# FFN up projection from seven block products instead of eight, with h split at the down projection

## The chip, the cores and the metric

The kernel runs on one core of one Trainium2 chip, in one launch. The metric is the device time of the launch in microseconds (us). A core has a matrix engine (TensorE, PE in the rows), a vector engine (VectorE, DVE), an activation engine (ScalarE, ACT), a general engine (GpSimd, POOL) and a queue that issues loads (SyncE, SP). Each runs its own instructions in the order in which they were put down; semaphores order them against each other. SBUF is the memory that all engines read and write, PSUM the one that matrix products land in.

## The reference, cut to what matters

The reference is one layer of a hybrid decoder for 512 prompt tokens and 64 sample tokens (8 sequences of 8), 576 tokens in all. The change touches only the gated feed-forward network (FFN) at its end:

```python
def conv_ffn(xn, conv_prev, w_up, conv_w, conv_b, w_down):
    t_len = xn.shape[1]
    a, b = jnp.split(xn @ w_up, 2, axis=-1)
    ext = jnp.concatenate([conv_prev.astype(a.dtype), a], axis=1)
    y = conv_b + conv_w[0] * ext[:, 0:t_len] + conv_w[1] * ext[:, 1:t_len + 1] + conv_w[2] * ext[:, 2:t_len + 2]
    h = jax.nn.silu(y) * b
    return h @ w_down, ext[:, -(CONV_WIDTH - 1):]
```

`xn` is the normalized [576, 1024] activation, `w_up` is [1024, 5632], `w_down` [2816, 1024], all FP32. The second result, the last two columns of `a` of each sequence, is an output too. A final norm follows.

## The kernel before

**Products.** FP32 precision comes from splitting each operand into a high part (`hi`, rounded to the matrix format fp32r) and the rest (`lo`), and adding three products: hi by hi, hi by lo, lo by hi. So each block of 128 rows by 128 columns of a weight costs three matmuls per token range, with the weight block as stationary operand and the tokens as moving operand. ScalarE makes the high part (L161), VectorE subtracts it from the raw weight for the rest (L164). A chunk of weights is one load by SyncE into `wr` (three buffers), usually 1024 by 128: eight blocks, one tile of 128 partitions by 1024. Its parts `wh` and `wl` have two buffers each. `fetch(i)`, called as chunk i begins, cuts chunks i and i+1 and loads i+2 and i+3.

**The stage before.** After the merge of the three mixers and the output projection, `x1` holds the residual; `xh2`, `xl2` its split, times the norm's gain but without the norm's factor for each token, `rst`. That factor is known only some 10 us after the first FFN matmul; so it is applied to the products.

**FFN up.** 2816 columns are 22 pairs: 128 gate columns `a`, 128 value columns `b`. For each f of the 22, `gemm` runs `a` over two token ranges (SPLIT, 256 and 320 tokens) and `b` over two of 288 (EVEN): 8 blocks, 3 products and 2 ranges each, 96 matmuls for a pair. VectorE takes `a` out of PSUM times `rst` into `ae` (L1159, L1161); the width-3 convolution is three VectorE instructions over 592 columns (L1184 to L1186), ScalarE applies SiLU (L1187), GpSimd multiplies by `rst` into `yr` (L1189, L1190), VectorE multiplies by `b` from PSUM (L226), and the result is split at once: `hh` on ScalarE (L1194), `hl` on VectorE (L1195). GpSimd also keeps the last columns of `a` (L1170, L1171) and issues behind them one copy of a cache within DRAM (L183), the side copies.

**FFN down.** For each of 8 blocks of 128 output columns, `down` (L1249) runs over the 22 blocks of h in three chunks (8, 7, 7 blocks), two token ranges side by side; the last block runs its ranges one after the other, so that the end can begin early. Transposes, the final norm and the output follow.

The order on each engine is the order of the code; a few instructions are put elsewhere by hand with `issue_after`. In the up loop the cut of the next chunk, called by `fetch`, stands in VectorE's order between the instructions that take results out.

## Time and profile before

| | us |
|---|---|
| median of 3 runs | 1325.38 (1325.1 to 1326.37) |
| span of the profiled execution | 1324.9 |
| the profiled execution outside its span | about 0.5 |
| PE busy | 1305.0 (99%) |
| DVE, ACT, POOL busy | 601.6, 464.3, 242.4 |
| first FFN up matmul starts | 886.99 |
| first FFN down matmul starts | 1171.16 |

The span is what the profiler saw from the first to the last instruction. The time of a run is taken around the program, and the median stands about 0.5 us above the span. A group row ("L164 DVE ... x43 | 52.6, 1222") gives line, engine, operation, output and inputs with their shapes, count, then busy time in us and mean duration of one in ns, and after a second bar the idle time of the engine just before these instructions and what ended it. A timeline row gives start, duration, engine, line and operation. PE instructions overlap: a matmul's own duration (297 ns) is longer than the distance from one to the next, and it is that distance which counts for time.

### The profile page before, as it was taken

The numbers are of one execution on the slowest core, as the hardware profiler recorded it, in microseconds if no ns is written. First come the engines' busy times: TensorE is split into PE (matmuls) and PEld (weight loads), VectorE is DVE, ScalarE is ACT, GpSimd is POOL, SyncE is SP. The second block draws the span as 40 slices with busy tenths as digits, with TensorE's granted clock in tenths as the row PEclk, the third lists the DMA queues.
The fourth block names the chain that finished last, engine by engine and source line by source line (L and its number), as shares of the span: only waits on it lengthen the run. The fifth ranks groups of instructions, "written<-read, shape, count | busy, mean of one in ns | idle before, by whom it ended". The sixth has DMA issues, their size and how long they took to land.

```text
span 1324.9 us, 23686 instructions
## 1 busy us (share of the span) xinstructions
PE 1305.0 (99%) x9903; PEld 1257.5 (95%) x9903; DVE 601.6 (45%) x1004; ACT 464.3 (35%) x899; POOL 242.4 (18%) x398
## 2 busy tenths in 40 slices
PE   8899999999999999999999999999999999999997
PEld 6899999999999999998988889999999999999997
DVE  5754564433453333162633366435555555532223
ACT  6554553534321222242433343433222222222223
POOL 4320211022410112041311110122121212200000
PEclk9999999999999999999999999999999999999999
DMA  7232432355443557266676415363455555444333
GB/s 218 65 116 68 144 115 69 96 178 158 131 141 95 163 159 220 73 184 190 182 217 204 154 31 167 100 225 118 145 164 162 162 167 157 148 129 149 91 88 116
DMA packets 220582, 187.44 MB, mean 141 GB/s; under 512 B 7900, under 2 KB 216393, under 8 KB 219700
## 3 DMA queue, kind: packets, MB, share of 16 engines
...
q8 instruction: 78, 1.28, 0.4%
...
q10 hardware_dynamic: 2, 0.00, 0.0%
...
## 4 chain that ended last, share of the span: by engine, by line
PE 94%; DVE 2%; ACT 2%; issue 1%; DMA 1%; POOL 0%; SPq 0%; POOLq 0%; DVEq 0%; ACTq 0%
PE g L207 63%; PE g L1249 8%; PE g L395 8%; PE h L1249 2%; PE h L936 1%; PE s L805 1%; PE s L207 1%; PE s L864 1%; PE s L828 1%; PE s L820 1%; PE s L881 1%; PE h L869 1%; PE s L611 0%; DVE bb L475 0%; PE s L591 0%
## 5 line engine op out<-in xcount | busy, mean ns | idle before, releaser
L207 PE MATMUL g<-xl,wh 128*128 128x288 f32 (+2 forms) x1664 | 494.1, 297 | 0.0
L207 PE MATMUL g<-xh,wh 128*128 128x288 f32 (+2 forms) x1664 | 494.1, 297 | 0.0
L207 PE MATMUL g<-xh,wl 128*128 128x288 f32 (+2 forms) x1664 | 492.8, 297 | 1.1 <-DVE wl L164 1.1
L161 ACT CAST wh<-wr 128x1024 fp32r<-128x1024 f32 (+3 forms) x181 | 184.4, 1019 | 485.8 <-PE g L207 287.8
L164 DVE TENSOR_TENSOR wl<-wr,wh 128x1024 fp32r<-128x1024 f32 (+3 forms) x179 | 227.1, 1268 | 252.9 <-ACT wh L161 252.2
L207 PEld LDWEIGHTS g<-xh,wl 128*128 128x128 f32 x1664 | 313.7, 189 | 3.3 <-issue 1.4
L207 PEld LDWEIGHTS g<-xl,wh 128*128 128x128 f32 x1664 | 314.1, 189 | 2.3 <-issue 2.0
L207 PEld LDWEIGHTS g<-xh,wh 128*128 128x128 f32 x1664 | 314.2, 189 | 1.1 <-issue 0.7
L395 PE MATMUL g<-wh,xh 128*128 128x256 f32 x224 | 72.1, 323 | 2.5 <-DVE vs L400 2.5
L1249 PE MATMUL g<-hh,wl 128*128 128x288 f32 (+2 forms) x286 | 72.2, 297 | 0.0
L1249 PE MATMUL g<-hh,wh 128*128 128x288 f32 (+2 forms) x286 | 72.0, 297 | 0.0
L395 PE MATMUL g<-wl,xh 128*128 128x256 f32 x224 | 71.5, 319 | 0.0
L1249 PE MATMUL g<-hl,wh 128*128 128x288 f32 (+2 forms) x286 | 71.5, 295 | 0.0
L395 PE MATMUL g<-wh,xl 128*128 128x256 f32 x224 | 71.4, 320 | 0.0
L395 PEld LDWEIGHTS g<-wh,xh 128*128 128x128 f32 x224 | 52.3, 233 | 5.7 <-DVE vs L400 2.7
L395 PEld LDWEIGHTS g<-wl,xh 128*128 128x128 f32 x224 | 52.3, 234 | 0.7 <-issue 0.7
L395 PEld LDWEIGHTS g<-wh,xl 128*128 128x128 f32 x224 | 52.4, 234 | 0.0
L1249 PEld LDWEIGHTS g<-hh,wl 128*128 128x128 f32 x286 | 49.8, 189 | 0.0
L1249 PEld LDWEIGHTS g<-hh,wh 128*128 128x128 f32 x286 | 49.6, 189 | 0.0
L1249 PEld LDWEIGHTS g<-hl,wh 128*128 128x128 f32 x286 | 49.6, 189 | 0.0
L1159 DVE TENSOR_TENSOR ae<-g,rst 128x256 f32<-128x256 f32 x44 | 18.6, 425 | 64.0 <-PE g L207 64.0
L226 DVE TENSOR_TENSOR yr<-yr,g 128x288 f32<-128x288 f32 x44 | 18.1, 451 | 49.8 <-POOL yr L1189 49.8
...
## 6 DMA issues: line engine op xcount, KB each, us to landing
...
```

Source lines behind the costliest of these rows:

```text
L161: S.copy(hi[:, :n], self.raw[:, :n])
L164: self.cut_at = E.tensor_tensor(lo[:, :n], self.raw[:, :n], hi[:, :n].bitcast(F32), op=OP.subtract)
L207: T.matmul(ps[:, :t1 - t0], a[:, k, c:c + 128], b(n)[:, t0:t1], start=(n == 0 and j == 0), stop=(n == len(ks) - 1 and j == 2))
L226: return lambda ps, t0, t1: V.tensor_tensor(t[:, t0:t1], t[:, t0:t1], ps, op=OP.mult)
L395: mm = T.matmul(dst, a, b[:, n % 4, :], start=(n == 0 and j == 0), stop=(n == 7 and j == len(seq) - 1))
L805: T.matmul(sp[:, nk * n:nk * n + nk], qT[r, p, 128 * t:128 * t + 128], kT[r, p, k0:k0 + nk], start=True, stop=True)
L820: T.transpose(pt[:, 128 * n:128 * n + 128], s4[:, h, 128 * kb:128 * kb + 128], ident)
L828: T.matmul(po[64 * hh:64 * hh + 64, 128 * x:128 * x + 128], vt[:, blocks[kb], 64 * (2 * p + hh):64 * (2 * p + hh) + 64], pts[:, (2 * x + h ...
L864: T.transpose(pk[:, 128 * n:128 * n + 128], kt[:, 2 * half + n // 2, 128 * (n % 2):128 * (n % 2) + 128], ident)
L869: T.matmul(sp[32 * b:32 * b + 32, 0:128], qz[:, p, 32 * b:32 * b + 32], kT[:, n, p, :], start=(r == 0 and p == 0), stop=(r == NR[g] - 1 an ...
L1159: V.tensor_tensor(ae[:, 2 + t0:258 + t0], ps[:, :256], rst[:, t0:t0 + 256], op=OP.mult)
L1249: T.matmul(q[:, :t1 - t0], a[:, k, :], b[n][:, t0:t1], start=(n == 0 and j == 0), stop=(n == NF - 1 and j == 2))
```

## The change

The gate and value columns of one pair form a 2 by 2 block matrix: the rows of the weight are split into blocks 0 to 3 and 4 to 7, the columns into `a` and `b`. The tokens are split into two halves of 288. The [tokens] by [rows] times [rows] by [columns] product then has eight block products, and in Winograd's form of Strassen's method it needs seven, with sums before and after:

- **Two plain pairs.** The first two pairs (NF0 = 2) stay as they were, but for the convolution's first step, which moves to ScalarE. Beside them `sums_x`, called four times for two block rows each, forms the seven combinations of x. They hold the norm's factor `rst` already (`scalar_tensor_tensor` with gain and `rst`, 2 instructions of 576 columns a call); two sums each on GpSimd and VectorE, seven high parts on ScalarE, seven rests on VectorE, all 288 wide.
- **20 pairs as units.** For each unit GpSimd forms the weight sums t1 to t4 (128 by 512 each). `part` cuts seven weight operands of 512 columns: high part on ScalarE (L147), rest on VectorE (L149), each into one of four buffers, three products ahead. A product is 4 blocks by 3 matmuls of 288 tokens: 12; seven are 84 for a pair, against 96. The seven products stay in PSUM and are combined: copies s1, s5 on ScalarE, five sums on VectorE with one operand from PSUM (L1334 to L1341, L1344, L1345), one of 288 from SBUF on GpSimd (L1339).
- **h.** GpSimd multiplies SiLU by `hb` into an FP32 h (L1349, L1350); the split into `hh` and `hl` moves behind the last up product: 22 high parts on ScalarE (L1359), 22 rests, 17 on VectorE and 5 on GpSimd (L1360).
- **Everywhere** weights are cut in tiles of 512 columns with four buffers each instead of 1024 with two. Raw weight chunks of the units alternate between `wr` and a second pool. The down projection (L1415) runs its first two output blocks third by third, side by side.

VectorE's order for one pair. Before (`wr`, `wh`, `wl` are raw weight, high part and rest; `ae` the extended gate column, `yr`, `hh`, `hl` the result and its split):

```order
L164 TENSOR_TENSOR wl<-wr,wh 128x1024
L1195 TENSOR_TENSOR hl_9576<-yr,hh_9554 128x576
L1159 TENSOR_TENSOR ae<-g,rst_9537 128x256 x2
L1161 TENSOR_TENSOR ae<-g,rst_9537 128x8x8
L1184 TENSOR_SCALAR y<-ae,fvec 128x592
L164 TENSOR_TENSOR wl<-wr,wh 128x1024
L1185 SCALAR_TENSOR_TENSOR y<-ae,fvec,y 128x592
L1186 SCALAR_TENSOR_TENSOR y<-ae,fvec,y 128x592
L226 TENSOR_TENSOR yr<-yr,g 128x288 x2
```

And with the change, from the second half of one unit into the next (`ts` is a weight sum, `g` and `s` are PSUM, `u`, `v`, `w`, `hb` the running sums):

```order
L1340 TENSOR_TENSOR ae<-u,g 128x288
L149 TENSOR_TENSOR wl<-ts,wh 128x512
L1341 TENSOR_TENSOR hb<-v,s 128x288
L149 TENSOR_TENSOR wl<-ts,wh 128x512
L1344 TENSOR_TENSOR ae<-w,g 128x224
L1345 TENSOR_TENSOR ae<-w,g 128x8x8
L149 TENSOR_TENSOR wl<-ts,wh 128x512
L1260 SCALAR_TENSOR_TENSOR y<-ae,fvec,y 128x592
L149 TENSOR_TENSOR wl<-wr,wh 128x512
L1261 SCALAR_TENSOR_TENSOR y<-ae,fvec,y 128x592
L1334 TENSOR_TENSOR u<-u,s 128x288
L149 TENSOR_TENSOR wl<-wr,wh 128x512
```

The rests of the weights, two a pair before and seven now, stand between the sums that empty PSUM and the two convolution steps; the split of h and the first convolution step are gone from here.

GpSimd's order for one pair. Before:

```order
L1170 COPY cc<-ae 128x2
L1171 COPY cc<-ae 128x16
L183 DMA out_dram<-in_cache_k_w_dram 32x16320
L1189 TENSOR_TENSOR yr<-y,rst_9537 128x512
L1190 TENSOR_TENSOR yr<-y,rst_9537 128x64
```

With the change:

```order
L1339 TENSOR_TENSOR hb<-w,s_11866 128x288
L1217 TENSOR_TENSOR ts<-wr 128x512
L1217 TENSOR_TENSOR ts<-wr,ts 128x512
L1279 COPY cc<-ae 128x2
L1280 COPY cc<-ae 128x16
L201 DMA out_dram<-in_cache_v_w_dram 32x16320
L1217 TENSOR_TENSOR ts<-wr 128x512
L1268 MEMSET ae 128x2
L1269 COPY ae<-fvec 128x8x2
L1349 TENSOR_TENSOR h_10391<-y,hb 128x512
L1350 TENSOR_TENSOR h_10391<-y,hb 128x64
L1217 TENSOR_TENSOR ts<-wr,ts 128x512
```

Four weight sums and one sum of a result stand between what was there before.

ScalarE's order at the end of the up projection, with the change (`cst` holds the last columns of `a`, transposed):

```order
L147 CAST wh<-wr 128x512 x4
L1259 ACTIVATE y<-ae,fvec 128x592
L1286 COPY cst<-s 18x128
L1262 ACTIVATE y<-y 128x592
L1359 CAST hh_13670<-h_9975 128x576
L1359 CAST hh_13671<-h_9976 128x576
```

All 22 high parts of h stand behind the last SiLU; before, each stood within its own pair.

The diff, cut to its core:

```diff
+NF0 = 2
...
+    def cut_part(src, E):
+        n = src.shape[1]
+        hi = wpool.tile([128, PART], F32R, tag="wh", name="wh", bufs=4)
+        S.copy(hi[:, :n], src)
+        lo = wpool.tile([128, PART], F32R, tag="wl", name="wl", bufs=4)
+        return hi, lo, E.tensor_tensor(lo[:, :n], src, hi[:, :n].bitcast(F32), op=OP.subtract)
...
-            hi = wpool.tile([128, WSLOT], F32R, tag="wh", name="wh", bufs=2)
-            S.copy(hi[:, :n], self.raw[:, :n])
-            lo = wpool.tile([128, WSLOT], F32R, tag="wl", name="wl", bufs=2)
-            E = G if self in chunks[:2] else V
-            self.cut_at = E.tensor_tensor(lo[:, :n], self.raw[:, :n], hi[:, :n].bitcast(F32), op=OP.subtract)
-            self.hi = hi[:, :n].rearrange("p (k c) -> p k c", k=self.kt)
-            self.lo = lo[:, :n].rearrange("p (k c) -> p k c", k=self.kt)
+            self.parts = []
+            for a in range(0, n, PART):
+                hi, lo, self.cut_at = cut_part(self.raw[:, a:min(a + PART, n)], G if self in chunks[:2] else V)
+                self.parts.append((hi, lo))
...
+    ORDER = ("11", "t2", "t1", "t3", "21", "22", "t4")
+    x_parts = {n: [sx.tile([128, 4, HALF], F32R, name=f"x{part}_{n}") for part in ("h", "l")] for n in ORDER}
+    f32 = lambda t: t.bitcast(F32)
...
+    def sums_x(k):
+        top, bottom = (fp.tile([128, NT], F32, tag="hb", name="xn", bufs=2) for _ in range(2))
+        for t, m in ((top, k), (bottom, k + 4)):
+            V.scalar_tensor_tensor(t, x1[:, m, :], vecs[:, m, 1:2], rst, op0=OP.mult, op1=OP.mult)
+        a11, a21, a12, a22 = top[:, :HALF], top[:, HALF:], bottom[:, :HALF], bottom[:, HALF:]
+        s3 = fp.tile([128, HALF], F32, tag="u", name="s3", bufs=2)
+        s2 = fp.tile([128, HALF], F32, tag="v", name="s2", bufs=2)
+        s4 = fp.tile([128, HALF], F32, tag="u", name="s4", bufs=2)
+        G.tensor_tensor(s3, a11, a21, op=OP.subtract)
+        V.tensor_tensor(a21, a21, a22, op=OP.add)
+        V.tensor_tensor(s2, a21, a11, op=OP.subtract)
+        G.tensor_tensor(s4, a12, s2, op=OP.subtract)
+        for n, x in (("11", a11), ("t2", s2), ("t1", a21), ("t3", s3), ("21", a12), ("t4", a22), ("22", s4)):
+            hi, lo = x_parts[n]
+            S.copy(hi[:, k], x)
+            V.tensor_tensor(lo[:, k], x, f32(hi[:, k]), op=OP.subtract)
...
+        def sum(self, *names):
+            b11, b21, b12, b22 = (c.raw[:, h:h + PART] for c in (self.a, self.b) for h in (0, PART))
+            t = self.sums
+            for n in names:
+                t[n] = sx.tile([128, PART], F32, tag="ts", name="ts", bufs=4)
+                p, q, op = {"t1": (b12, b11, OP.subtract), "t2": (b22, t.get("t1"), OP.subtract),
+                            "t3": (b22, b12, OP.subtract), "t4": (b21, t.get("t2"), OP.subtract)}[n]
+                G.tensor_tensor(t[n], p, q, op=op)
...
+    AHEAD = 3
+    def prepare(u, p):
+        if p == 0 and u + 1 < len(units):
+            units[u + 1].load()
+        if p == 2 and u + 1 < len(units):
+            units[u + 1].sum("t1", "t2")
+        if p == 4 and u + 1 < len(units):
+            units[u + 1].sum("t3", "t4")
+        for n in range(7 * u + p, min(7 * u + p + AHEAD + 1, 7 * len(units))):
+            units[n // 7].part(ORDER[n % 7])
+        if 7 * u + p + AHEAD >= 7 * len(units):
+            fetch(P["dn", 0][0])
+    def product(u, p):
+        prepare(u, p)
+        ps = big() if p % 2 == 0 else small()
+        n = ORDER[p]
+        (wh, wl), (xh, xl) = units[u].parts[n], x_parts[n]
+        for k in range(4):
+            for j, (a, b) in enumerate(((wh, xh), (wh, xl), (wl, xh))):
+                T.matmul(ps[:, :HALF], a[:, 128 * k:128 * k + 128], b[:, k, :], start=(k == 0 and j == 0), stop=(k == 3 and j == 2))
+        return ps[:, :HALF]
...
+    def conv(f, ae):
+        y = fp.tile([128, 592], F32, tag="y", name="y", bufs=1)
+        S.activation(y, ae[:, 0:592], AF.Identity, scale=fvec[:, f, 16:17], bias=fvec[:, f, 19:20])
+        V.scalar_tensor_tensor(y, ae[:, 1:593], fvec[:, f, 17:18], y, op0=OP.mult, op1=OP.add)
+        V.scalar_tensor_tensor(y, ae[:, 2:594], fvec[:, f, 18:19], y, op0=OP.mult, op1=OP.add)
+        S.activation(y, y, AF.Silu)
+        return y
...
-        y = fp.tile([128, 592], F32, tag="y", name="y", bufs=1)
-        V.tensor_scalar(y, ae[:, 0:592], fvec[:, f, 16:17], fvec[:, f, 19:20], op0=OP.mult, op1=OP.add)
-        V.scalar_tensor_tensor(y, ae[:, 1:593], fvec[:, f, 17:18], y, op0=OP.mult, op1=OP.add)
-        V.scalar_tensor_tensor(y, ae[:, 2:594], fvec[:, f, 18:19], y, op0=OP.mult, op1=OP.add)
-        S.activation(y, y, AF.Silu)
-        yr = fp.tile([128, NT], F32, tag="yr", name="yr", bufs=2)
...
+        sums_x(2 * f)
...
-        S.copy(h_hi[f], yr)
-        V.tensor_tensor(h_lo[f], yr, h_hi[f].bitcast(F32), op=OP.subtract)
+        sums_x(2 * f + 1)
+        if f == NF0 - 2:
+            units[0].load()
+        if f == NF0 - 1:
+            units[0].sum("t1", "t2", "t3", "t4")
+            for n in ORDER[:AHEAD]:
+                units[0].part(n)
...
+        s1, s5, v, w = part("u"), part("s5", 1), part("v"), part("w", 1)
+        S.copy(s1, product(u, 0))
+        p6 = product(u, 1)
+        u2 = part("u")
+        V.tensor_tensor(u2, s1, p6, op=OP.add)
+        p5 = product(u, 2)
+        S.copy(s5, p5)
+        V.tensor_tensor(v, u2, p5, op=OP.add)
+        V.tensor_tensor(w, u2, product(u, 3), op=OP.add)
+        G.tensor_tensor(hb[:, HALF:], w, s5, op=OP.add)
+        V.tensor_tensor(ae[:, 2:2 + HALF], s1, product(u, 4), op=OP.add)
+        V.tensor_tensor(hb[:, :HALF], v, product(u, 5), op=OP.add)
+        p4 = product(u, 6)
+        n = NP - HALF
+        V.tensor_tensor(ae[:, 2 + HALF:2 + NP], w[:, :n], p4[:, :n], op=OP.add)
+        V.tensor_tensor(aes[:, :, 2:10], by_sample(w[:, n:]), by_sample(p4[:, n:]), op=OP.add)
+        keep_state(f, ae, aes)
+        y = conv(f, ae)
+        h = hs[f]
+        G.tensor_tensor(h[:, :NP], y[:, :NP], hb[:, :NP], op=OP.mult)
+        G.tensor_tensor(by_sample(h[:, NP:]), by_sample(y[:, 512:592])[:, :, 2:10], by_sample(hb[:, NP:]), op=OP.mult)
...
+    for f in range(NF):
+        S.copy(h_hi[f], hs[f])
+        (G if f % 4 == 3 else V).tensor_tensor(h_lo[f], hs[f], f32(h_hi[f]), op=OP.subtract)
...
+    ps = [[big(), big()], [big(), small()]]
+    n = [0, 0]
+    for t in range(3):
+        for m in range(2):
+            n[m] = down(m, P["dn", m][t:t + 1], ps[m], EVEN, n[m])
+            if t == 2:
+                add_down(m, ps[m], EVEN)
+                rows_out(m, range(5))
+                side_copy(G.tensor_copy(pace, x1[:, m, 0:1]))
...
```

162 lines of the change are left out of this document (110 added, 52 removed).

## Prediction

> **What bounds the kernel now.** I read the page first: which engine is busy, and which ends the chain of waits.
>
> ```profile
> span 1324.9 us, 23686 instructions
> PE 1305.0 (99%) x9903; PEld 1257.5 (95%) x9903; DVE 601.6 (45%) x1004; ACT 464.3 (35%) x899; POOL 242.4 (18%) x398
> ...
> PE 94%; DVE 2%; ACT 2%; issue 1%; DMA 1%; POOL 0%; SPq 0%; POOLq 0%; DVEq 0%; ACTq 0%
> ```
>
> PE bounds. Is that so in the stage that changes? The view of windows gives one stretch of the up projection (the columns are PE, PEld, DVE, ACT, POOL busy, granted clock, DMA share):
>
> ```profile
> 915.00:940.00 25.00, 25.00 (x191) 25.00 (x190) 13.96 (x22) 6.74 (x8) 4.84 (x15) 1.00 0.57 174
> ```
>
> It is: PE without a gap at full clock, VectorE 56% busy, GpSimd 19%. So fewer matmuls are time saved, as long as the others deliver in the shorter period. A matmul's price is the distance between starts in the timeline of PE:
>
> ```profile
> 941.30 0.27 PE L207 MATMUL g<-xh,wh 128*128 128x256 f32 x1
> ...
> 947.68 0.29 PE L207 MATMUL g<-xh,wh 128*128 128x288 f32 x1
> ...
> 954.04 0.27 PE L207 MATMUL g<-xh,wh 128*128 128x256 f32 x1
> ```
>
> From `a` of one pair to `a` of the next are 12.74 us; its 48 matmuls of 288 take 954.04 - 947.68 = 6.36, 0.1325 each. A unit of 84 takes 11.13 us. **PE's saving**: 20 x (12.74 - 11.13) = 32.2 us, the most that the change can bring.
>
> **What the helpers must do in 11.13 us.** Groups of the up stage (before the bar busy us and mean ns):
>
> ```profile
> L164 DVE TENSOR_TENSOR wl<-wr,wh 128x1024 fp32r<-128x1024 f32 x43 | 52.6, 1222 | 12.8 <-ACT wh L161 12.7
> L1189 POOL TENSOR_TENSOR yr<-y,rst 128x512 f32<-128x512 f32 x22 | 28.1, 1277 | 18.7 <-ACT y L1187 18.7
> L1159 DVE TENSOR_TENSOR ae<-g,rst 128x256 f32<-128x256 f32 x44 | 18.6, 425 | 64.0 <-PE g L207 64.0
> L1186 DVE SCALAR_TENSOR_TENSOR y<-ae,fvec,y 128x592 f32<-128x592 f32 x22 | 18.4, 835 | 0.8
> L226 DVE TENSOR_TENSOR yr<-yr,g 128x288 f32<-128x288 f32 x42 | 17.3, 452 | 47.5 <-POOL yr L1189 47.5
> L1195 DVE TENSOR_TENSOR hl<-yr,hh 128x576 fp32r<-128x576 f32 x21 | 15.8, 752 | 0.0
> L1187 ACT ACTIVATE y<-y 128x592 f32<-128x592 f32 x22 | 15.4, 698 | 53.0 <-DVE y L1186 52.6
> L1194 ACT CAST hh<-yr 128x576 fp32r<-128x576 f32 x21 | 14.1, 671 | 1.3 <-DVE yr L226 1.3
> L183 POOL DMA_DIRECT2D out_dram<-in_cache_v_w_dram x11 | 6.1, 556 | 0.4
> L1190 POOL TENSOR_TENSOR yr<-y,rst 128x64 f32<-128x64 f32 x21 | 6.4, 307 | 0.0
> L1161 DVE TENSOR_TENSOR ae<-g,rst 128x64 f32<-128x64 f32 x22 | 4.7, 215 | 0.0
> L1171 POOL COPY cc<-ae 128x16 f32<-128x16 f32 x22 | 4.3, 197 | 0.0
> ```
>
> *VectorE, a unit*: seven rests of 512 (between 576 in 752 ns and 1024 in 1222, a line gives 685 ns) 4.8 us; two convolution steps 1.67; six sums from PSUM, five of 288 at most (0.45) and L1344's 224 (0.40), with L1345 0.21: 2.87. Together 9.3 us, 84%. *GpSimd*: five operations of 512 (four weight sums, h) at 1.277, 6.39; h of the samples 0.31; the 288-wide sum 0.78 by the line through 64 and 512; three copies 0.6; the issue of a side copy about 0.55 and a memset: 8.7 us, 78%. *ScalarE*: seven high parts below 0.67, two copies of PSUM, two activations of 0.70: at most 6.9 us. Each fits alone.
>
> **Together they do not.** Elsewhere in this trace VectorE and GpSimd split a tensor between them (L1085); at 883 us a lone GpSimd operation of that size runs beside a VectorE one with an operand in PSUM (L1115). First VectorE's rows of the timeline and L1115's group, then GpSimd's with the view of the tile `ocl` (min, median, max ns):
>
> ```profile
> 788.55 0.76 DVE L1085 TENSOR_TENSOR ocl<-oun,och 128x576 fp32r<-128x576 f32 x1 [0.46 <-ACT och L1084]
> 789.71 3.44 DVE L1085 TENSOR_TENSOR ocl<-oun,och 128x576 fp32r<-128x576 f32 x2 [0.40 <-ACT och L1084]
> 793.07 2.18 DVE L164 TENSOR_TENSOR wl<-wr,wh 128x768 fp32r<-128x768 f32 x1
> 883.99 0.46 DVE L1115 SCALAR_TENSOR_TENSOR x<-g,x 128x288 f32<-128x288 f32 x1 [0.96 <-PE g L207]
> L1115 DVE SCALAR_TENSOR_TENSOR x<-g,x 128x288 f32<-128x288 f32 x16 | 7.3, 458 | 29.4 <-PE g L207 29.4
> ```
>
> ```profile
> 789.17 5.26 POOL L1085 TENSOR_TENSOR ocl<-oun,och 128x576 fp32r<-128x576 f32 x3 [35.84 <-ACT och L1084]
> 883.19 1.42 POOL L1124 TENSOR_TENSOR sq<-sq,sq 128x576 f32<-128x576 f32 x1 [5.59 <-ACT sq L1120]
> L1085 POOL TENSOR_TENSOR ocl<-oun,och x3: 1437/1939/1959, 789.2 to 792.5; 128x576 fp32r<-128x576 f32 x3
> ```
>
> A subtraction that takes VectorE 0.76 alone takes 1.72 beside GpSimd's; GpSimd's go from 1.42 to 1.95. One of each takes 1.95 us, 90% of the sum alone (1.42 + 0.76 = 2.18): they run in turns. With an operand in PSUM, L1115 keeps its 0.46 beside GpSimd (the group's mean is 458 ns) and GpSimd its 1.42. In the up stage of before nothing meets: VectorE waits 47.5 us for `yr`, idle, whenever GpSimd multiplies.
>
> The Trainium skill states this as a rule (page "SBUF — State Buffer", section "Who interferes with whom"): a VectorE instruction with two SBUF inputs and a GpSimd one that reads SBUF share a port pair as an exclusive lock, one SBUF input does not contend. The rows agree on both points, and the rule speaks against this change. Taken at its word, for whole instructions, it would make the sum of the next part 13.95 us a unit and the time some 20 us longer than mine; the rows' 90% is what I use.
>
> **The steady period.** Taking turns per unit: GpSimd 6.39 + 0.31 + 0.78 = 7.48, VectorE's rests and convolution steps 4.8 + 1.67 = 6.47; 13.95 x 0.9 = **12.55 us**, above PE's 11.13. VectorE's 2.87 us from PSUM can run beside GpSimd. Bounds: 12.3 if GpSimd's 64-wide piece counts for nothing; 12.55 + 2.87 = 15.4 if nothing is hidden. In VectorE's order the rests alternate with sums that wait for PE, so much is hidden; but GpSimd's sum L1339 waits for `w`, its h for SiLU, and the weight sums stand behind them: at times neither holds the turn. I add 0.3: **12.85**, near the lower end since both queues hold work ahead (operands three products, weight sums most of a unit). Over the 19 units after the first: 19 x (12.85 - 11.13) = **+32.7 us**.
>
> **The start.** `sums_x` needs the norm's factor; the last operands of unit 0 need its fourth call.
>
> ```profile
> 896.90 0.59 ACT L1141 COPY rst<-s 128x512 f32<-128x512 f32 x1
> 915.80 0.27 PE L207 MATMUL g<-xh,wh 128*128 128x256 f32 x1
> 1171.16 0.29 PE L1249 MATMUL g<-hh,wh 128*128 128x288 f32 x1
> ```
>
> `rst` is there at 897.5; PE ends the second pair at 915.8 and could end unit 0 at 926.9. VectorE until then: 8 products of 576 with `rst` (0.82, as the convolution's steps), 6.6; 8 sums and 28 rests of 288, 0.45 each, 16.2; two pairs' results and convolutions 2 x (1.07 + 1.67 + 0.9) = 7.3; about six rests of weights 4.1: 34 us. GpSimd: 8 sums of 0.78, two `yr` of 1.58, four weight sums of 1.28: 14.5. Of VectorE's 34 some 30 take turns: (30 + 14.5) x 0.9 = 40, its sums from PSUM beside. So the operands are whole at 897.5 + 40 = 937.5; the last two products (24 x 0.1325 = 3.2) follow, 940.7: **+13.8 us**; without turns 897.5 + 34 + 3.2 gives 934.7, +7.8.
>
> **The end.** Before, h is split pair by pair, and down follows at 1171.16 without a gap. Now ScalarE makes the 22 high parts behind the last SiLU; the first rest is there some 6 us after the last up matmul (two sums, convolution 0.70 + 1.67, SiLU 0.70, high part 0.67, rest 0.76, each with a hand-over). Then 17 rests on VectorE take turns with 5 on GpSimd: (17 x 0.752 + 5 x 1.42) x 0.9 = 17.9, so 23.9 us after. Behind them in VectorE's order stands the rest of the third weight chunk of down. PE has two chunks until there, 96 matmuls and the first of the next: 13.7 us. **+10 us**, without turns 6 + 12.8 - 13.7 = +5.1.
>
> The rest of the edits I cost at nothing: 512-wide cuts elsewhere add one operation of about 0.1 us per chunk, in an engine 45% busy with chunks cut one ahead, under the 6.4 us that PE spends on a chunk; uncovered, some 137 chunks would cost 14 us. The bytes and the number of loads are the same, and SyncE's queue holds little but loads; side copies are issued as often.
>
> **Sum**, on the profiled 1324.9 span and 0.5 around it (the median of the runs is the same 1325.4): 1325.4 - 32.2 + 32.7 + 13.8 + 10 = 1349.7, **1349 us**. With period 12.3 to 13.5, start 10 to 17 and end 8 to 11 the forecast runs from 1333 to 1366.
>
> **Rivals.**
> *PE stays the bound* (0.17): GpSimd's operations fall into VectorE's waits for PE, as `yr` does today. For it: each engine fits alone (84%, 78%). Against it: 12.55 us of turns in 11.13 must meet; it needs turns of below 80% of the sum, while the rows show 90%. 1325.4 - 32.2 + 7.8 + 5.1 = 1306.
> *In between* (0.09): period 11.9, because copies into the engines' queues overlap more; start 8, end 6: 1325.4 - 32.2 + 14.6 + 14 = 1322.
> *A convoy* (0.12): the loop sum L1339, SiLU, h, weight sum, rest, product closes on itself; then part of VectorE's PSUM sums stands in it too. From half of the 2.87 on it decides: 12.85 + 1.4 = 14.2, 19 x 3.07 = 58: 1325.4 - 32.2 + 58 + 24 = 1375. Against it: products are cut three ahead.
> *The change doesn't remove what it says*: PE's order shows 84 matmuls a unit; I give it nothing.
> *The clock*: in the first 50 us a stretch of idling is followed by a lower clock:
>
> ```profile
> 44.00:48.00 4.00, 1.71 (x15) 1.51 (x13) 4.00 (x5) 0.78 (x2) 3.00 (x2) 1.00 0.00 0
> 48.00:52.00 4.00, 3.76 (x23) 3.77 (x24) 4.00 (x7) 3.01 (x5) 3.89 (x5) 0.71 0.00 0
> ```
>
> In the waits at start and end that may add 1 to 2 us, inside the range; in the steady part PE idles 1.7 us of each 12.85, in pieces.
>
> **How the numbers follow.** Forecast 0.62, in between 0.09, PE bound 0.17, convoy 0.12. A difference of 0.2% (2.7 us) is what can be told from none. Faster: PE bound and 0.04 of in between, 0.21; same 0.04; slower 0.75. For eight in ten the range takes all of the forecast and of in between, and some of either outer case: 1311 to 1372; the forecast's own is 1333 to 1366.
>
> **What would show it.** Right: the rests L149 take well over 685 ns in the mean, near 1.1 to 1.4 us, GpSimd's L1217 well over 1277, while VectorE's sums from PSUM keep 452; PE idles, released by VectorE's `wl`, some 1.7 us a unit; the first down matmul stands 24 us or so later than before, less 10 of it at the end. Wrong: L149 at about 690 ns and PE at 99% between units; or PE waiting for loads, ScalarE or PSUM buffers in place of `wl`. The start is wrong if unit 0 ends before 935, the end if the wait in front of down's third chunk is under 5 us.

## The result and the profile after

| | before | after |
|---|---|---|
| median (4 runs each, side by side) | 1325.62 (1325.1 to 1326.37) | 1366.72 (1365.64 to 1368.75) |
| span of the profiled execution | 1324.9 | 1364.2 |

The changed kernel is slower: ratio 1.0307, 95% interval 1.0293 to 1.0322. The forecast was 1349 with 1311 to 1372; the direction and the range hold, the size is 17 us short, and the time lies just above the 1333 to 1366 that the forecast gave for itself. The medians differ by 41.1 us and the spans by 39.3: wherever one execution has both, its time stands some 1.8 us above its span, so the 0.5 us given for before compares the span of one execution with the median of others. The accounts below are in span. The page after:

```profile
span 1364.2 us, 24416 instructions
PE 1298.1 (95%) x9663; PEld 1238.9 (91%) x9663; DVE 770.0 (56%) x1296; ACT 567.3 (42%) x1226; POOL 425.3 (31%) x513
```

TensorE has 240 matmuls less and is busy only 7 us less, and it no longer fills the span. The share of VectorE, 56%, is an average that hides the stage. Windows of the up projection alone, after (columns as in the prediction: PE, PEld, DVE, ACT, POOL busy, granted clock, DMA share, GB/s):

```profile
947.00:1197.00 250.00, 226.36 (x1589) 217.50 (x1587) 237.14 (x302) 114.79 (x211) 204.06 (x223) 0.97 0.48 151
```

and the same stage before:

```profile
927.00:1171.00 244.00, 244.00 (x1840) 243.96 (x1840) 132.72 (x209) 65.23 (x81) 51.35 (x130) 1.00 0.52 157
```

VectorE is busy 95% of the stage and GpSimd 82%, where the forecast's work alone would have made 84% and 78% of a much shorter one; TensorE idles 23.6 of 250 us and its clock, 1.00 before, is 0.97. The groups of the stage tell why the two are so busy (VectorE's rests of raw weights and of weight sums, a sum out of PSUM, then GpSimd's weight sums):

```profile
L149 DVE TENSOR_TENSOR wl<-ts,wh 128x512 fp32r<-128x512 f32 x79 | 92.1, 1166 | 2.9 <-ACT wh L147 2.8
...
L149 DVE TENSOR_TENSOR wl<-wr,wh 128x512 fp32r<-128x512 f32 x59 | 66.5, 1128 | 0.0
L1217 POOL TENSOR_TENSOR ts<-wr 128x512 f32<-128x512 f32 x38 | 57.0, 1500 | 13.5 <-DMA wr<-in_ffn_w_up_dram 7.5 <-DVE wl L149 3.4 <-ACT wh L147 2.3
L1217 POOL TENSOR_TENSOR ts<-wr,ts 128x512 f32<-128x512 f32 x38 | 54.4, 1432 | 9.5 <-DVE wl L149 8.7
...
L1340 DVE TENSOR_TENSOR ae<-u,g 128x288 f32<-128x288 f32 x19 | 8.4, 443 | 0.9 <-PE g L1254 0.9
```

A rest takes 1.13 to 1.17 us where 0.685 was the price alone; GpSimd's sums 1.43 to 1.50 for 1.28; a VectorE sum with an operand in PSUM keeps its 0.44. The two convolution steps, whose operands are both in SBUF, go the same way: 1.32 us each between 947 and 1197 us, 0.835 before. These are the marks that the prediction named for turns, and all three are there. TensorE's waits over the whole program, with total, count and longest:

```profile
PE s L1254 <- DVE wl L149: 10.3, 7, 3.9
PE g L1415 <- ACT hh L1359: 5.6, 1, 5.6
PE g L1254 <- DVE wl L149: 5.5, 6, 1.8
PE s L1284 <- POOL cc L1280: 5.2, 2, 3.9
PE g L226 <- DVE h L245: 5.2, 1, 5.2
PE h L1254 <- DVE wl L149: 3.7, 4, 1.6
```

Most of it is for `wl` (L1254), as forecast: 19.5 us. Two entries were not: 5.2 us for GpSimd's copies of the kept columns (L1280, in front of their transposes on TensorE, L1284), and 5.2 us at the start for L245, of which more below.

**Where the 39.3 us of span came from.** The Identity, ScalarE's activation L1259, is the first step of a unit's convolution. Those of the first and of the last unit (ScalarE's timeline) give the period:

```profile
946.60 0.89 ACT L1259 ACTIVATE y<-ae,fvec 128x592 f32<-128x592 f32 x1 [0.43 <-DVE ae L1345]
...
1197.79 0.88 ACT L1259 ACTIVATE y<-ae,fvec 128x592 f32<-128x592 f32 x1
```

251.2 us over 19 units are 13.22 each. An Identity starts some 0.8 us after its unit's last matmul (the very last one ends at 1197.1), so unit 0 ends at 945.8. The accounts, by the prediction's own terms:

| term | forecast | measured | how measured |
|---|---|---|---|
| TensorE's saving | -32.2 | -32.2 | 20 x 1.61; the period without a wait is 11.11 in the first experiment |
| ahead of the FFN | 0 | -1.9 | `rst` written from 895.00 instead of 896.90 |
| start | +13.8 | +20.9 | unit 0 ends 945.8, TensorE alone 926.9 - 1.9 = 925.0 |
| steady, 19 units | +32.7 | +39.7 | 13.22 against 11.13 |
| end | +10 | +13.4 | last up matmul to the end of the span: 1364.2 - 1197.1 = 167.1, before 1324.9 - 1171.16 = 153.7 |
| sum | +24.3 | +39.9 | span: +39.3 |

So no term had the wrong sign, and each of the three losses was too small in the forecast: by 7.1, 7.0 and 3.4 us.

### The profile page after: what moved, and what is told of

Read it like the earlier page. It is cut to its first block, busy times and chain, and to the rows that moved or that the text cites. A ratio compares the mean times of both kernels' runs of the same rounds, so it can differ in the third digit from the quotient of the medians.

```text
span 1364.2 us, 24416 instructions
## 1 busy us (share of the span) xinstructions
PE 1298.1 (95%) x9663; PEld 1238.9 (91%) x9663; DVE 770.0 (56%) x1296; ACT 567.3 (42%) x1226; POOL 425.3 (31%) x513
## 3 DMA queue, kind: packets, MB, share of 16 engines
q8 instruction: 76, 1.25, 0.4%
## 5 line engine op out<-in xcount | busy, mean ns | idle before, releaser
L149 DVE TENSOR_TENSOR wl<-wr,wh 128x512 fp32r<-128x512 f32 x334 | 260.0, 780 | 325.8 <-ACT wh L147 320.6
L147 ACT CAST wh<-wr 128x512 fp32r<-128x512 f32 x338 | 204.8, 608 | 351.9 <-PE g L226 224.8
L226 PE MATMUL g<-xh,wh 128*128 128x288 f32 (+2 forms) x1024 | 306.6, 299 | 5.2 <-DVE h L245 5.2
L226 PE MATMUL g<-xh,wl 128*128 128x288 f32 (+2 forms) x1024 | 306.0, 299 | 0.0
L226 PE MATMUL g<-xl,wh 128*128 128x288 f32 (+2 forms) x1024 | 305.0, 298 | 0.0
L226 PEld LDWEIGHTS g<-xh,wh 128*128 128x128 f32 x1024 | 194.2, 190 | 8.2 <-DVE h L245 5.4
L226 PEld LDWEIGHTS g<-xl,wh 128*128 128x128 f32 x1024 | 194.1, 190 | 1.4 <-issue 1.1
L226 PEld LDWEIGHTS g<-xh,wl 128*128 128x128 f32 x1024 | 194.1, 190 | 1.0 <-issue 0.6
L149 DVE TENSOR_TENSOR wl<-ts,wh 128x512 fp32r<-128x512 f32 x80 | 92.8, 1160 | 2.9 <-ACT wh L147 2.8
L1415 PE MATMUL g<-hh,wh 128*128 128x288 f32 (+2 forms) x286 | 71.5, 301 | 5.6 <-ACT hh L1359 5.6
L1415 PE MATMUL g<-hh,wl 128*128 128x288 f32 (+2 forms) x286 | 71.4, 299 | 2.9 <-DVE wl L149 2.9
L1415 PE MATMUL g<-hl,wh 128*128 128x288 f32 (+2 forms) x286 | 71.0, 298 | 0.2 <-DVE hl L1360 0.2
L147 ACT CAST wh<-ts 128x512 fp32r<-128x512 f32 x80 | 48.7, 617 | 48.0 <-PE g L1254 19.9
L1217 POOL TENSOR_TENSOR ts<-wr 128x512 f32<-128x512 f32 x40 | 60.1, 1502 | 17.1 <-DMA wr<-in_ffn_w_up_dram 11.1
L1415 PEld LDWEIGHTS g<-hh,wh 128*128 128x128 f32 x286 | 49.5, 191 | 5.8 <-ACT hh L1359 5.8
L1254 PE MATMUL g<-xh,wl 128*128 128x288 f32 x160 | 49.7, 311 | 4.5 <-DVE wl L149 3.7
```

Source lines behind the costliest of these rows:

```text
L147: S.copy(hi[:, :n], src)
L149: return hi, lo, E.tensor_tensor(lo[:, :n], src, hi[:, :n].bitcast(F32), op=OP.subtract)
L226: T.matmul(ps[:, :t1 - t0], a, b(n)[:, t0:t1], start=(n == 0 and j == 0), stop=(n == len(ks) - 1 and j == 2))
L1217: G.tensor_tensor(t[n], p, q, op=op)
L1254: T.matmul(ps[:, :HALF], a[:, 128 * k:128 * k + 128], b[:, k, :], start=(k == 0 and j == 0), stop=(k == 3 and j == 2))
L1415: T.matmul(q[:, :t1 - t0], a, b[n][:, t0:t1], start=(n == 0 and j == 0), stop=(n == NF - 1 and j == 2))
```

## The experiments

All are edits of the changed kernel unless said otherwise. "Period" is the mean distance of the units' Identities; "late" is how far the first of them lies behind where TensorE alone would put it (925.8 with two plain pairs, 12.74 more with each further pair). Each run had the kernel before beside it, at 1325.6 to 1327.3 us. Where no range is given the time is that of one run.

| kernel | us | first Identity, late | period |
|---|---|---|---|
| after | 1366.72 | 946.6, 20.8 | 13.22 |
| no_sums | 1316.92 | 939.8, 14.0 | 11.11 |
| sums_dve | 1335.37 | 944.1, 18.3 | 11.67 |
| light_pool | 1371.0 | 948.6, 22.8 | 13.47 |
| copy_mid | 1364.13 | 946.9, 21.1 | 13.20 |
| light_mid | 1356.13 | 947.2, 21.4 | 12.74 |
| start (4 plain pairs) | 1352.61 | 966.1, 14.8 | 12.85 |
| end | 1358.8 | 946.9, 21.1 | 12.98 |
| best0 (4) | 1334.84 | 964.6, 13.3 | 12.18 |
| best1 (4) | 1332.87 | 965.3, 14.0 | 11.92 |
| best2 (6) | 1324.06 | 986.5, 9.7 | 11.70 |

### Is it the weight sums on GpSimd?

The theory was turns: VectorE's instructions with two operands in SBUF and GpSimd's that read SBUF run one after the other. The rival was that VectorE's load, its order, or the loads of weights set the period. The first run leaves the weight sums out, so that the cuts take raw blocks and the products are not those of Winograd's form:

```diff
-                G.tensor_tensor(t[n], p, q, op=op)
+                t[n] = {"t1": b12, "t2": b22, "t3": b12, "t4": b21}[n]
```

> The changed kernel without GpSimd's four weight sums: the cuts of t1 to t4 take a raw block of the weight in their place, so this run leaves the sums out and computes other numbers with the same cuts and products. Turns (VectorE's instructions with two SBUF operands and GpSimd's reads exclude each other): GpSimd keeps about 2.4 us of turns a unit, with VectorE's 6.5 well below PE's 11.13, so the period falls from 13.2 to about 11.2 and PE bounds; 19 x 2.0 = 38 us less, and some 4 us at the start, where four sums go too: 1320 to 1330. The rests fall from a mean of 1.16 us to 0.7 to 0.8. Rival, VectorE too loaded by itself (its order of rests between sums that wait for PE): VectorE's work is unchanged, so the period stays within 0.5 us of 13.2 and the time above 1355.

Measured: 1316.92 us. The window from 990 to 1150 us and the rests of its up stage:

```profile
990.00:1150.00 160.00, 160.00 (x1212) 159.90 (x1210) 129.78 (x231) 92.98 (x159) 67.32 (x111) 1.00 0.56 173
```

```profile
L149 DVE TENSOR_TENSOR wl<-wr,wh 128x512 fp32r<-128x512 f32 x143 | 105.8, 740 | 14.5 <-ACT wh L147 11.1
```

TensorE has no gap, the clock is 1.00, the rests are back at 740 ns and every unit takes 10.8 to 11.2 us. The change's saving is real and is all there in the steady part once these 80 instructions are gone. That does not yet tell turns from mere work: the sums are work too. The second run therefore keeps every one of them and gives them to the engine that is already 95% busy:

```diff
-                G.tensor_tensor(t[n], p, q, op=op)
+                V.tensor_tensor(t[n], p, q, op=op)
```

> The changed kernel with the four weight sums on VectorE instead of GpSimd: the same work, moved to the engine that is already 95% busy. VectorE's own work goes from 9.3 to 9.3 + 4 x 0.685 = 12.0 us a unit, GpSimd's falls by 5.1. Turns: (6.5 + 2.7 + 2.4) x 0.9 = 10.4 us, no longer the bound; the period is VectorE's own 12.0 to 12.6 and the time 1366 - 19 x 0.6 to 1.2 = 1343 to 1355, faster than the change. Rival, VectorE's load: 2.7 us more on the bound, period near 15, time near 1400.

Measured: 1335.37 us, 31 us faster than the changed kernel and better than the theory's own range. Its groups in the up stage:

```profile
L149 DVE TENSOR_TENSOR wl<-ts,wh 128x512 fp32r<-128x512 f32 x80 | 69.0, 864 | 0.1
L149 DVE TENSOR_TENSOR wl<-wr,wh 128x512 fp32r<-128x512 f32 x63 | 48.5, 769 | 0.4 <-ACT wh L147 0.4
L1217 DVE TENSOR_TENSOR ts<-wr,ts 128x512 f32<-128x512 f32 x38 | 30.5, 801 | 0.0
L1217 DVE TENSOR_TENSOR ts<-wr 128x512 f32<-128x512 f32 x38 | 26.6, 700 | 2.6 <-DMA wr<-in_ffn_w_up_dram 1.4 <-DVE wl L149 1.2
```

VectorE does a sum in 0.70 to 0.80 us. On GpSimd it cost 1.43 to 1.50 us, and the rests beside it took 1.13 to 1.17 in place of the 0.77 to 0.86 here. More work on the busier engine made the kernel faster: a period set by the mere amount of VectorE's work would have become longer. This is the run that decides between the two. A third cause would be GpSimd's own queue, 82% busy, delivering its sums late. Both runs take the sums out of that queue, so they do not exclude it; the changed kernel's trace speaks against it: VectorE idles only 12.9 of the 250 us, and nearly all of TensorE's waits are for VectorE's rests.

### The same effect in the kernel before

If turns are a matter of the two engines alone, GpSimd work that nobody needs must slow the kernel before too, as far as it meets VectorE; memory fills, which read nothing, must not.

```diff
+        for _ in range(5 if 4 <= f < 18 else 0):
+            if f < 11:
+                G.tensor_tensor(dc, x1[:, 0, :NP], x1[:, 1, :NP], op=OP.add)
+            else:
+                G.memset(dc, 0.0)
```

> The kernel before, with idle work for GpSimd that nobody waits for, behind the convolution of a pair: in pairs 4 to 10 five sums of two SBUF tiles (128 by 512), in pairs 11 to 17 five fills of such a tile, which read nothing. Turns: in pairs 4 to 10 the rests L164 (1222 ns alone) that fall beside the sums take up to 2.4 us, and GpSimd's sums go from 1.28 to some 1.7; in pairs 11 to 17 the rests keep 1222 ns. VectorE has room in a pair of 12.74 us (7 us busy), so the time stays within 0.3% of before. If the slow rests of the changed kernel had another cause than GpSimd's reads (weights just loaded, 512-wide tiles, PSUM), the rests here keep 1222 ns in both.

Measured: 1340.43 us, 13.8 more than the kernel before beside it: a miss. In the trace the sums ran earlier than written, in one stretch from 891 to 971 us, the fills from 972 to 997. The groups of the stretch with sums:

```profile
L1191 POOL TENSOR_TENSOR dc<-x 128x512 f32<-128x512 f32 x25 | 36.2, 1449 | 1.2
...
L164 DVE TENSOR_TENSOR wl<-wr,wh 128x1024 fp32r<-128x1024 f32 x7 | 12.3, 1756 | 5.3 <-ACT wh L161 5.3
...
L1196 POOL TENSOR_TENSOR yr<-y,rst 128x512 f32<-128x512 f32 x3 | 5.8, 1924 | 0.0
L1186 DVE TENSOR_SCALAR y<-ae,fvec 128x592 f32<-128x592 f32 x4 | 5.5, 1372 | 0.1
```

and, with the fills (their group, then the two rests that lie wholly beside fills):

```profile
L1193 POOL MEMSET dc<- 128x512 f32 x35 | 18.4, 527 | 1.6
```

```profile
982.55 1.22 DVE L164 TENSOR_TENSOR wl<-wr,wh 128x1024 fp32r<-128x1024 f32 x1
...
994.56 1.23 DVE L164 TENSOR_TENSOR wl<-wr,wh 128x1024 fp32r<-128x1024 f32 x1 [0.47 <-DMA out_dram<-cst]
```

The slowing itself is as the theory has it: a rest of 1024 takes 1756 ns in the mean beside sums, up to 2.73 us, and keeps its price of 1222 beside fills. The forecast of no change was wrong because the slowing reached TensorE. Between 891 and 971 us it waited 8.7 us, in five pieces, for the instruction that takes `b` out (L226), and pairs took up to 16.6 us instead of 12.74. Ahead of L226 stood `yr` (L1196), behind a sum in GpSimd's order or slowed itself (1924 ns), and a slowed rest on VectorE, 2.13 us for one at 937.2. Three stretches at a lower granted clock make up the remaining 5 us or so (0.93 and 0.95 in the mean of 887 to 927 and 927 to 972 us).

One row was not expected at all: L1186 has only one operand in SBUF, yet it took 1.62, 1.63 and 1.65 us beside sums, and 0.59 where it met none. The Trainium skill (page "SBUF — State Buffer", section "Who interferes with whom") has an exception that fits: `tensor_scalar` can enter a mode that takes both ports, if its operands meet certain conditions, and can contend then. The trace agrees with the exception, and the prediction had used only the rule.

### Lightening GpSimd, and what stood in its way

If 8.7 us of GpSimd a unit are too much, giving back its small operations should help: the 288-wide sum L1339 to VectorE out of PSUM, three small copies to ScalarE.

```diff
-        G.tensor_tensor(hb[:, HALF:], w, s5, op=OP.add)
+        V.tensor_tensor(hb[:, HALF:], w, p5, op=OP.add)
...
-        G.memset(ae[:, 0:2], 0.0)
-        G.tensor_copy(aes[:, :, 0:2], fvec[:, f, 0:16].rearrange("p (b n) -> p b n", b=8))
+        side_copy(G.memset(ae[:, 0:2], 0.0))
+        S.copy(aes[:, :, 0:2], fvec[:, f, 0:16].rearrange("p (b n) -> p b n", b=8))
```

> The changed kernel with less on GpSimd: the 288-wide sum L1339 goes to VectorE with its operand straight from PSUM (0.45 us, no turn), which drops a copy on ScalarE; the copies of the kept columns and of the convolution state go to ScalarE. Turns: GpSimd loses the 1.26 us of L1339 and the three copies that cost 0.6, 0.56 and 0.36 each in the changed kernel, 2.8 us of 13.2; the period falls to 11.2 to 12.0, the time to 1366 - 19 x 1.2 to 2.0 = 1328 to 1343. Rival, VectorE's load: VectorE gets 0.45 us more, the period rises or stays: 1366 to 1375.

Measured: 1371.0 us, slower than the changed kernel: a miss. GpSimd did less and waited instead, for loads of raw weights (its waits), behind a SyncE queue in which the kept columns' 14 small outputs stand ahead of the next load (timeline of that queue, first and last):

```profile
POOL ts L1217 <- DMA wr<-in_ffn_w_up_dram: 59.4, 9, 12.3
```

```profile
1006.32 0.43 SPq L1289 DMA_DIRECT2D out_dram<-cst  x1
...
1018.19 0.32 SPq L1290 DMA_DIRECT2D out_dram<-cst  x1
1018.60 3.05 SPq L163 DMA_DIRECT2D wr<-in_ffn_w_up_dram  x3
```

The edit had moved the side copies, of up to 2 MB, to another moment as well (`side_copy` hangs on another instruction). So two runs took that apart: copy_mid moves only the side copies, behind the second weight sum; light_mid is light_pool with the copies there.

> The changed kernel with the side copies of the units issued behind the second weight sum, in the middle of a unit, instead of behind the kept columns at its end, so that a 2 MB copy no longer stands in front of the next unit's loads. If late loads make the long units of the changed kernel (15 to 16.6 us where most take 12 to 13), they go: some 10 us less, 1354 to 1358. Turns, with GpSimd's bursts making the long units: GpSimd waits only 3.9 us for loads in the changed kernel, so the time stays at 1362 to 1369.

> The lighter GpSimd of the earlier run (sum L1339 on VectorE from PSUM, small copies on ScalarE) together with the side copies behind the second weight sum. In the earlier run the copies had moved to where the loads are issued, and GpSimd waited 53.5 us for loads. If those waits hid the gain, the period now falls to 11.9 to 12.4 and the time to 1340 to 1352. If lighter turns bring nothing (VectorE's own load bounds), it stays at 1364 to 1375.

Measured: 1364.13 and 1356.13 us. The copies' place alone is worth 2.6 us, about what can be told from none; with it, lightening GpSimd gives 8 us more and a period of 12.74, some 4 us short of the theory's range. Light_mid and light_pool differ in the copies' place alone, so of light_pool's time that place cost 14.9 us; the 14 outputs are the same in both. Nor is light_mid free of late loads: GpSimd waits 28.9 us for them from 940 to 1205 us, against 53.5 in light_pool and 7.5 in the changed kernel, so what lighter turns alone would give stays open. The operations taken from GpSimd had 2.8 us a unit in the changed kernel's trace (L1339 1.26, the copies 0.61, 0.56 and 0.36), and the unit shortens by 0.46; the four sums had 5.9 and gave 1.55, even though VectorE must do them.

### The start and the end

`start` makes four plain pairs instead of two and calls `sums_x` once a pair instead of twice, so that 18 units have its work ahead of them:

```diff
-NF0 = 2
+NF0 = 4
...
-        sums_x(2 * f)
...
-        sums_x(2 * f + 1)
+        if f < 4:
+            sums_x(f)
```

> The changed kernel with four plain pairs instead of two and one call of sums_x a pair instead of two: the same preparation of x spread over twice the time, 18 units instead of 20. Start set by VectorE's preparation taking turns: its 34 us of VectorE work now has 51 us of PE work beside it; the lateness of the first unit (14 to 20 us in the changed kernel) falls below 4. Two pairs run at 12.74 instead of 13.22. 1366 - 11 to 17 = 1349 to 1355. If the first unit is late for another reason (weights, PSUM), 1363 to 1367.

Measured: 1352.61 us, as expected, 14.1 less. But the reason was only in part the one given. The first unit is still 14.8 us late (20.8 without the edit), a gain of 6.0; two units fewer lose 3.2 of TensorE's saving; and what the periods have above 11.13 falls from 39.7 us (19 periods) to 29.2 (17 of 12.85), a gain of 10.5. Part of what keeps the start late is in the waits, TensorE for VectorE taking out a plain pair:

```profile
PE g L226 <- DVE h L245: 6.1, 2, 3.2
```

Instructions of `sums_x` stand in VectorE's order ahead of the one that empties PSUM. No_sums fits: without any weight sum on GpSimd it still starts 14.0 us late.

`end` makes 22 rests on VectorE, none on GpSimd, seven of them behind the cut of down's third chunk, and gives the output buffer `cst` a second copy:

```diff
-            cst_o = fp.tile([126, 128], F32, tag="cst", name="cst", bufs=1)
+            cst_o = fp.tile([126, 128], F32, tag="cst", name="cst", bufs=2)
...
-    for f in range(NF):
-        S.copy(h_hi[f], hs[f])
-        (G if f % 4 == 3 else V).tensor_tensor(h_lo[f], hs[f], f32(h_hi[f]), op=OP.subtract)
+    def split_h(fs):
+        for f in fs:
+            S.copy(h_hi[f], hs[f])
+            V.tensor_tensor(h_lo[f], hs[f], f32(h_hi[f]), op=OP.subtract)
+
+    split_h(range(15))
```

> The changed kernel with a second buffer for the kept columns' output (ScalarE waited 4.25 us for it ahead of the last SiLU), all 22 rests of h on VectorE (no turns with GpSimd there) and the last seven splits of h behind the cut of the third chunk of down. The wait before down falls from 7.2 us after the last up product to 3 to 4, the wait for the third chunk (2.9) goes, and PE runs without holes after: 6 to 9 us less, 1357 to 1361. If the end's cost lies in the number of splits alone (16.5 us of VectorE work), 1363 to 1367.

Measured: 1358.8 us, 7.9 less, as expected. All rests on VectorE:

```profile
L1362 DVE TENSOR_TENSOR hl<-h,hh 128x576 fp32r<-128x576 f32 x22 | 15.8, 788 | 4.2 <-ACT hh L1361 4.1
```

A rest takes 0.79 us here; beside GpSimd's five, 17 of them took 18.5 us, 1.09 each. All 22 on one engine are 15.8 us of work, less than the 17 were: GpSimd's help was none. The three edits were not tried one by one.

### All repairs together

best0 joins the edits of sums_dve, start and end; best1 adds L1339 out of PSUM on VectorE.

> The same without the move of L1339: GpSimd adds 288 columns of two SBUF tiles a unit (0.8 to 1.26 us) and ScalarE copies its operand out of PSUM. Turns: 0.3 to 0.4 us more a unit than the kernel with the move, 5 to 7 us in all. If VectorE's own load bounds, this kernel has 0.37 us less on VectorE a unit and is 5 to 7 us faster than with the move.

> The parts that worked, together: weight sums on VectorE, sum L1339 on VectorE straight from PSUM, four plain pairs with one sums_x each, the end's three edits. Turns: GpSimd keeps only the product h and small copies, so the period is VectorE's own: 11.67 as with the sums alone, less up to 0.4 for L1339, over 17 periods; the first unit comes some 12 us less late, the end 8 us earlier, two more plain pairs cost 2 x 1.2. From 1335.4: 1335.4 - 10 to 12 - 8 - 0 to 6 + 2.4 = 1312 to 1320, faster than the kernel before (1325.5). If the gains overlap (the start's lateness was already smaller with the sums on VectorE), 1320 to 1327.

Measured: 1334.84 us and 1332.87 us (5 runs, 1331.2 to 1334.6), ratio of best1 to before 1.0046 (1.0032 to 1.0060): both a miss, best1 by some 13 us. Moving L1339 is worth 0.26 us a unit (12.18 and 11.92). Three stalls of TensorE of 2 to 3 us remain at the start, two of them with a lower clock behind them, as in this window (no gap in it, and 24 matmuls in 5 us instead of 38):

```profile
942.00:947.00 5.00, 5.00 (x24) 5.00 (x25) 1.51 (x3) 0.82 (x2) 1.54 (x2) 0.66 0.63 253
```

and in best0 every third unit is long (13.1 to 13.9 us), with VectorE's sums waiting for loads of weights (8.1 us in five waits). So the last kernel, made from best1, spreads the sums of x in halves over six plain pairs, cuts the 2 MB side copy in two, and writes the kept columns' outputs two a pair:

```diff
-NF0 = 4
+NF0 = 6
...
+    def write_late(n):
+        for _ in range(min(n, len(late))):
+            nc.sync.dma_start(*late.pop(0))
...
+        if f:
+            next(halves, None)
...
-        if f < 4:
-            sums_x(f)
+        next(halves, None)
```

> The repaired kernel once more (weight sums and kept h/rest work on VectorE, fewer waits at the end), with three edits against what its trace still showed: 6 instead of 4 plain pairs at the front, with the sums of x in halves spread over them, so that no clump of them stands ahead of an eviction; the 2 MB side copy in two halves; the kept column's outputs two per pair instead of 14 at once. Theory (the time above the kernel before came from three stalls of TensorE of some 3 us at the start, each with a lower granted clock behind it, and from weights that land late every third unit): 1315 to 1322 us, below the kernel before's 1325.6; the first Identity of unit 0 within 5 us of where TensorE alone would put it, the unit 11.5 to 11.8 us, no wait of TensorE over 2 us between the first plain pair and the last unit. Rival (VectorE's own load of 16 to 18 unit's worth of sums sets the period, whatever is ahead of it): the unit stays at 11.9 us or above and the time is 1328 us or more.

Measured: 1324.06 us (11 runs, 1321.91 to 1326.45) against 1327.34 (15 runs, 1325.57 to 1328.85); ratio 0.9975, interval 0.9966 to 0.9984. It is faster than the kernel before, by a quarter of a per cent, and short of the 1315 to 1322 expected. The period came as expected (11.70); waits over 2 us are gone behind the first plain pair; the first Identity is 9.7 us late instead of under 5. Its stretch from 990 to 1150 us:

```profile
990.00:1150.00 160.00, 155.38 (x1159) 153.40 (x1158) 157.51 (x288) 82.75 (x139) 61.95 (x100) 1.00 0.55 163
```

Here VectorE is 98% busy and GpSimd 39%: VectorE's own load is now the bound, 0.57 us a unit above TensorE. The rival was right on what limits the steady part, and wrong on the level. In span: 16 units save 25.8; 9.7 at the start, 15 x 0.57 = 8.6 in the steady part, about 8 at the end, and 1.9 gained ahead of the FFN leave -1.4, against -1.9 measured (1323.0 and 1324.9).

## Why the prediction was right, and where it was too small

**The mechanism and the direction: shown.** The step that decided was "together they do not": two engines, each below 85% by the forecast, that slow each other whenever both work from SBUF. No_sums and sums_dve confirm it from two sides, and before_pool shows the same slowing of single instructions in the other kernel. Two rivals fall, TensorE as the bound (1306) and the one in between (1322).

**The steady period: 12.85 forecast, 13.22 measured.** The starts and ends of all instructions between 947 and 1197 us show what the sum was made of. A rest or convolution step on VectorE, or a sum or product on GpSimd, is under way in 229.0 of these 250 us, 12.1 a unit. That is 88% of what the same instructions would take alone, one after the other (259, by the prediction's prices): the 90% was a good price, and the turns, forecast at 12.55, were no longer than that. What was mis-sized is the 0.3 us for times in which neither holds the turn: these are 21.0 us, 1.1 a unit.

The same reading deals with the convoy (1375, period 14.2), which is closer in time than the forecast. It needs half of VectorE's PSUM sums, 1.4 us a unit, to stand with no turn beside them. Of their 50.0 us, 34.8 run beside GpSimd's sums and products, as the prediction had it, and 15.2, or 0.8 a unit, do not. So a part of what the convoy says does happen, and it is most of the time that neither holds.

Of the 19 periods, five are 14.1 to 16.6 us long (76.4 us together); the other 14 have a mean of 12.48. Two of the five hold a rest that stood still, for 4.73 and 3.51 us; one has the wait of 3.87 us told below; the other two were not taken apart. In the worst, from 1021.5 to 1038.1 us, VectorE's timeline shows one rest of 4.73 us:

```profile
1027.03 4.73 DVE L149 TENSOR_TENSOR wl<-wr,wh 128x512 fp32r<-128x512 f32 x1
1031.68 0.80 DVE L149 TENSOR_TENSOR wl<-ts,wh 128x512 fp32r<-128x512 f32 x1
```

GpSimd's beside it:

```profile
1027.32 1.28 POOL L1217 TENSOR_TENSOR ts<-wr,ts 128x512 f32<-128x512 f32 x1
1028.56 1.26 POOL L1217 TENSOR_TENSOR ts<-wr 128x512 f32<-128x512 f32 x1
...
1029.80 0.19 POOL L1269 COPY ae<-fvec 128x16 f32<-128x16 f32 x1
1029.95 1.25 POOL L1349 TENSOR_TENSOR h<-y,hb 128x512 f32<-128x512 f32 x1
1031.17 0.76 POOL L1350 TENSOR_TENSOR h<-y,hb 128x64 f32<-128x64 f32 x1
```

and TensorE's:

```profile
1031.81 0.61 PE L1254 MATMUL s<-xh,wl 128*128 128x288 f32 x1 [3.90 <-DVE wl L149]
```

GpSimd runs three operations at full speed (1.25 to 1.28, its price alone) while the rest, begun earlier, stands still, and TensorE loses 3.9 us. Here the engines do not alternate: GpSimd, with its next instruction ready each time, keeps going. The prediction's rows held one or two instructions of a kind beside three of the other and could not show that.

On TensorE's side the forecast was "PE idles, released by VectorE's `wl`, some 1.7 us a unit". The idle time for `wl` in these 250 us is 19.8 us, 1.0 a unit, and 23.6 with the wait of 3.87. But TensorE's busy time grew as well: 250 us hold 18.9 units of 11.13, 210.5 us, and it was busy for 226.4. Most of these 15.9 us are waits too:

```profile
1049.07 0.29 PE L1254 MATMUL g<-xl,wh 128*128 128x288 f32 x1
1049.49 0.40 PE L1254 MATMUL g<-xh,wl 128*128 128x288 f32 x1
1049.73 0.29 PE L1254 MATMUL g<-xh,wh 128*128 128x288 f32 x1
```

The starts are 0.42 and 0.24 us apart where 0.13 is the rule. A matmul lasts 0.29 us, so a wait of up to 0.16 behind it shows as busy time. Outside the stretches with a granted clock of 0.50 there are 84 such distances, 0.15 to 0.40 us without the idle time, 82 of them beside a matmul that reads `wl`; they lose some 10 us. So the waits for `wl` cost 30 us, 1.6 a unit, and the 1.7 was nearly right. Their shape was not: three waits of 1.8 to 3.9 us lie among the small ones.

What the prediction put at nothing for the steady part is the clock. The other 5.9 us of the 15.9 are matmuls under a granted clock of 0.50: 54 of them took 13.0 us instead of 7.2. These lie in three stretches, which set in during or right behind the waits of 3.90, 3.87 and 2.69 us. The window with the hold has 0.86 in the mean (0.50 from 1031.1 to 1037.9):

```profile
1022.00:1047.00 25.00, 20.21 (x129) 19.64 (x129) 23.45 (x23) 10.15 (x20) 20.15 (x24) 0.86 0.49 169
```

Put at nothing were also the transposes of the kept columns. They wait in TensorE's order for GpSimd's small copies, and once, until 1095.9 us, TensorE stood there for 3.87 us.

**The start: 43.2 us after `rst` forecast, 50.2 measured (945.8 - 895.6).** The prediction summed VectorE's and GpSimd's work; it took TensorE's plain pairs as undisturbed. They were not:

```profile
909.39 0.63 PE L226 MATMUL g<-xh,wh 128*128 128x320 f32 x1 [5.21 <-DVE h L245]
921.91 0.29 PE L1254 MATMUL g<-xh,wh 128*128 128x288 f32 x1
```

L245, which empties PSUM, began at 908.9. The product that it needs from GpSimd was there at 906.7, so 2.2 of the 5.21 us belong to the instructions right ahead of it in VectorE's order, three of `sums_x` and one rest; for the others, that product itself came late. Waits for VectorE make 11.1 us between 897 and 947 us. Behind the 5.21 us the granted clock is 0.50 from 908.2 to 915.0, and behind two waits of 1.85 and 1.63 us (until 925.9 and 928.1) again from 928.7 to 942.3:

```profile
922.00:947.00 25.00, 19.15 (x97) 17.06 (x96) 23.79 (x41) 11.90 (x26) 11.18 (x12) 0.73 0.15 43
```

97 matmuls at 0.1325 are 12.9 us; TensorE took 19.15 for them. In both stretches together 63 matmuls took 16.9 us, some 8 more than at full clock. With the 11.1 us of waits that is most of the 20.9. So the start's term was short by a wait in TensorE's plain pairs and by the clock, of which the prediction had given "1 to 2 us" for start and end. Since the start stays 14.0 us late without the weight sums, turns with these are not the whole of it; how much is turns inside `sums_x` and how much is its order was not taken apart.

**The end: +10 forecast, +13.4 measured, and in another place.** The prediction put its wait in front of down's third chunk and said that under 5 us there would show it wrong. It is 2.87 (TensorE's timeline):

```profile
1198.50 0.28 PE L1284 MATMUL s<-ca,cc 128*18 128x128 f32 x1 [1.36 <-POOL cc L1280]
1204.39 1.09 PE L1415 MATMUL g<-hh,wh 128*128 128x288 f32 x3 [5.62 <-ACT hh L1359]
...
1223.53 0.54 PE L1415 MATMUL g<-hh,wl 128*128 128x288 f32 x2 [2.87 <-DVE wl L149]
```

Its 23.9 us of rests behind the last up matmul were about right (25.8: 7.3 until the first, then 18.50 for VectorE's 17), but the cover of 13.7 us was counted from that matmul on, as if the first two chunks did not have to wait. They do, for the first high parts, which stand on ScalarE behind this:

```profile
1202.93 0.25 ACT L1286 COPY cst<-s 18x128 f32<-18x128 f32 x1 [4.25 <-DMA out_dram<-cst]
1203.09 0.69 ACT L1262 ACTIVATE y<-y 128x592 f32<-128x592 f32 x1
```

The kept columns' output buffer, a single one, was still being written out, and the last SiLU and all 22 high parts stood behind it. 1.36 + 5.62 + 2.87 are 9.9 us of waiting. The granted clock is 0.50 from 1201.8 to 1208.6, and down's matmuls fill the last 4.2 us of that: an estimate of 2.1 more. The remaining 1.4 us were not resolved. That the total came within 3.4 us is in part luck, since the wait that it was priced by is not where the time went.

The first down matmul starts at 1204.4, 33.2 us later than before. The prediction's sign, "24 us or so later than before, less 10 of it at the end", was too small as its terms were.

**The clock over all three.** By these estimates TensorE lost some 8, 6 and 2 us to a lower clock, 16 together, where the prediction had 1 to 2. That is about what the forecast was short of. How much of it would have come back at a clock of 1.00 no run shows, since the operands were late as well.

**What cost nothing, as forecast:** the 512-wide cuts elsewhere. TensorE is busy 857 us of the first 870, as before, and `rst` is even 1.9 us earlier.
